# A two-block transformer stack on one core: queries and keys of the second block transposed together, doubled on the way out of PSUM

## The chip, the core and the metric

The kernel runs on one core of a Trainium2 chip. The time is the device time of one execution in microseconds (us), from three executions. The engines are TensorE (PE, with its weight loads PEld), VectorE (DVE), ScalarE (ACT), GpSimd (POOL) and SyncE (SP), which issues the DMAs. Each works through its own instructions in order and waits on semaphores for the others.

## The reference

512 tokens of width 1024 pass through a first block (two layers of feed-forward, mixing with differential attention, feed-forward) and a second block of two hybrid layers. Only the second block is touched:

```python
def hybrid_layer(x, mem, norm_g, w_in, w_out, mem_norm_g, w_mem_kv, qk_g):
    h = rms_norm(x, norm_g)
    proj = jnp.einsum('btd,de->bte', h, w_in)
    a_q, a_k, a_v, a_g, b_q, b_k, b_v, b_g, m_q, m_g = jnp.split(proj, cuts, axis=-1)
    qa = rope(rms_norm(to_heads(a_q, N_HEADS_MOBA), qk_g[0]))
    ka = rope(rms_norm(to_heads(a_k, N_HEADS_MOBA), qk_g[1]))
    oa = from_heads(moba_attention(qa, ka, to_heads(a_v, N_HEADS_MOBA)))
    ...   # b: six dilated heads, in the same way
    mkv = jnp.einsum('bmd,de->bme', rms_norm(mem, mem_norm_g), w_mem_kv)
    m_k, m_v = jnp.split(mkv, 2, axis=-1)
    qm = rms_norm(to_heads(m_q, N_HEADS_MEM), qk_g[4])
    km = rms_norm(to_heads(m_k, N_HEADS_MEM), qk_g[5])
    om = from_heads(memory_attention(qm, km, to_heads(m_v, N_HEADS_MEM)))
    y = jnp.concatenate([oa * jax.nn.silu(a_g), ob * jax.nn.silu(b_g), om * jax.nn.silu(m_g)], axis=-1)
    return x + jnp.einsum('bte,ed->btd', y, w_out)
```

There are 6 + 6 + 4 heads of 64 columns, 512 tokens, 256 memory rows. Every query and key is normalized over its 64 columns, the first twelve heads' are rotated, and the scores need them with the 64 columns on the partitions.

## The kernel before

**Precision.** Every matmul operand is kept as a float32r value ("hi") and the remainder ("lo"). A product takes three matmuls (`mm3`: hi by hi, hi by lo, lo by hi; lines 56 to 58). ACT makes the hi by a cast (`hi`, line 62), DVE or POOL the lo by a subtraction (`lo`, line 67). Weights come in tiles `wf` by DMA; ACT and POOL split each half tile into `wh` and `wl`, up to three halves ahead of PE.

**Second block.** x stands transposed in SBUF, in eight tiles of 128 channels by 512 tokens. A layer (`hyb`) is a list of steps, `HYB` (line 547): `u0` to `u5` are the rope units, each the queries and keys of two heads; `u6` the queries of the four memory heads; `v` a group of four heads' values, `g` a pair's gates, `m` the memory's keys and values, `A` to `C` a quarter of the output projection. The part ahead of the first bar runs alone; each later part is blended (`blend`) with the attention of one pair of heads, in the order of `PAIRS`: after every piece of attention a few pieces of steps follow. A unit step has four pieces, a gate step two.

**A unit** (`token_major`, then `put_unit`). 96 matmuls of 256 columns give, in two PSUM accumulators (tag `acc`, three buffers) of 512 columns, for four groups of 128 tokens the 256 columns q, k, q, k of two heads. `put_unit` then has, traced with priority: ACT copies both accumulators to SBUF (`u`, line 715). `heads` squares them on ACT (623), sums the squares per head on DVE (624), takes the power -1/2 on POOL (`qc`, 630), and for each half multiplies `u` by a table of cosines on DVE (`m`, 636) and by one of sines on POOL (`n`, 637), and adds the two on POOL (639). For each group of 128 tokens DVE multiplies by `qc` and writes each head's 64 columns twice side by side (`m2`, 648), PE transposes the four blocks of 128 columns (653) into a PSUM tile `pt` (tag `tp`, two buffers, shared with attention), and `unit_dest` takes it out: one cast by ACT for all four, one subtraction on DVE for the keys' lo (`kl`), one for the lower half of the queries. So a query stands as hi over lo on 128 partitions and a key as hi over hi, and two matmuls make a score.

The memory queries take the same way without the rotation (the gain is multiplied in on POOL, 642), the memory keys too, with 256 rows.

**What sets the order.** The program is traced through a framework that orders each engine's instructions by trace order, by priority and by its own estimate of times; buffers from a pool are handed out as they come free. Scratch tiles of 128x512 (tag `t`) have six buffers.

Of the kernel before, what the change touches and what calls it, by code (L numbers as in the profile page):

```python
# [11 lines left out]
F = _mybir.dt.float32  # L12
# [33 lines left out]
class Kernel:  # L46
# [500 lines left out]
    HYB = 'u0 v0 g0|u1 g1|m u6|g6 g7 u2|v1 g2 A|u3 g3|u4 v2|u5 g4 g5|B C'.split('|')  # L547
# [31 lines left out]
    def hyb(self, l, hp, stats, after, late):  # L579
# [36 lines left out]
        def heads(us, nt, zz, kind, gain, dest):  # L616


            nb = nt // 2
# [11 lines left out]
            for b, u in enumerate(us):  # L631
                if kind is not None:
                    co, si = (t[:, 2 * b:2 * b + 2].unsqueeze(2).to_broadcast([P, 2, 2, 128]) for t in tabs[kind])
                    u4 = u.rearrange("p (a b c) -> p a b c", a=2, b=2)
                    m, n = scratch("m"), scratch("n")
                    nc.vector.tensor_tensor(m.rearrange("p (a b c) -> p a b c", a=2, b=2), u4, co, op=ALU.mult)
                    nc.gpsimd.tensor_tensor(n.rearrange("p (a b c) -> p a b c", a=2, b=2), u4, si, op=ALU.mult)
                    m3, n3 = (x.rearrange("p (a s c) -> p a s c", s=2, c=32) for x in (m, n))
                    nc.gpsimd.tensor_tensor(m3, m3, n3[:, :, ::-1], op=ALU.add)  # L639
                else:  # L640
                    m = scratch("m")
                    nc.gpsimd.tensor_tensor(m.rearrange("p (a c) -> p a c", c=64), u.rearrange("p (a c) -> p a c", c=64),
                                            gain.unsqueeze(1).to_broadcast([P, 8, 64]), op=ALU.mult)
                m8 = m.rearrange("p (a c) -> p a c", c=64)
                for i in range(2):
                    h4 = slice(8 * b + 4 * i, 8 * b + 4 * i + 4)
                    m2 = scratch("m2")
                    nc.vector.tensor_tensor(m2.rearrange("p (a d c) -> p a d c", a=4, d=2),  # L648
                                            m8[:, 4 * i:4 * i + 4].unsqueeze(2).to_broadcast([P, 4, 2, 64]),
                                            c[:, h4].unsqueeze(2).unsqueeze(3).to_broadcast([P, 4, 2, 64]), op=ALU.mult)  # L650
                    pt = self.ps.tile([P, 4, P], F, tag="tp", name="pt", bufs=2)
                    for j in range(4):
                        nc.tensor.transpose(pt[:, j], m2[:, j * P:(j + 1) * P], self.ident)
                    dest(pt, 2 * b + i)

        def unit_dest(qk, kl):

            def f(pt, tt):
                t = slice(tt * P, (tt + 1) * P)
                self.hi(qk[:, :, t], pt)  # L660
                self.lo(nc.vector, kl[:, :, t], pt[:, 1::2], qk[:, 1::2, t])
                self.lo(nc.vector, qk[64:P, 0::2, t], pt[64:P, 0::2], qk[64:P, 0::2, t])
            return f

        def q_dest(qk):
            def f(pt, tt):
                t = slice(tt * P, (tt + 1) * P)
                self.hi(qk[:, :, t], pt)
                self.lo(nc.vector, qk[64:P, :, t], pt[64:P], qk[64:P, :, t])
            return f  # L670

        def k_dest(kh, kl):
# [4 lines left out]
            return f  # L677

# [31 lines left out]
        def put_unit(p):  # L710
            def f(pv):
                us = []
                for b in range(2):
                    u = scratch("u")
                    nc.scalar.copy(u, flat(pv[b]))  # L715
                    us.append(u)
                qk = hp.tile([P, 4, T], R, tag="qk", name="qk", bufs=2)
                if p < 6:
# [437 lines left out]
```

## Time and profile before

| | us |
|---|---|
| median of 3 executions | 2536.55 |
| lowest, highest | 2532.47, 2537.79 |
| the profiled execution | 2537.32 |
| its span | 2535.5 |
| PE busy in the span | 2443.4 (96%) |
| POOL, ACT, DVE busy | 1531.0, 1058.1, 932.3 |
| second block within the span | from about 1885 to 2535 |

The span is the time from the first to the last instruction. Busy time is the union of an engine's instructions. A row of waits says which engine's instruction stood idle and what ended that; a row of the timeline gives start, duration, engine, line, tile written and read, and in brackets the idle time ahead of it. PEclk is the clock that TensorE was granted, as a share of 2.4 GHz; 0.50 is its other level, 1.2 GHz.

### The profile page before, as it was taken

The page shows a single profiled execution, that of the slowest core. Times are in us where ns is not written, and L with a number is a line of the kernel's source. Part 1 is how long each engine was busy: PE and PEld are TensorE (multiplying, and loading weights), DVE is VectorE, ACT ScalarE, POOL GpSimd, SP SyncE. Part 2 cuts the span into 40 slices and gives each one's busy share as a digit, 9 for nine tenths or more (in the row PEclk, how much of TensorE's full clock was granted, in tenths as well). Part 3 has the DMA queues.
Part 4 walks back from the last instruction along what each step waited for, and adds up shares of the span by engine and source line. Part 5 has one row for each costly group of instructions (what it writes and reads, how often), then busy time and mean ns, then how long its engine had stood idle before and what let it go on. Part 6 is the DMA issues. An engine that isn't in the chain of part 4 may idle for free.

```text
span 2535.5 us, 32847 instructions
## 1 busy us (share of the span) xinstructions
PE 2443.4 (96%) x12390; PEld 2065.3 (81%) x12390; DVE 932.3 (37%) x1607; ACT 1058.1 (42%) x2009; POOL 1531.0 (60%) x1184
## 2 busy tenths in 40 slices
PE   8999999999999999999999999999997999889988
PEld 6888888887888888888888888888886888778886
DVE  3111114772111111111127841111165766765777
ACT  4333335643333333333336543333445554555553
POOL 7777555547666557666546377766655535555543
PEclk9999999999999999999999999999998999989999
DMA  3323332223333332333332223333332212122211
GB/s 127 100 92 100 92 110 92 81 73 94 98 100 96 93 100 93 100 95 94 97 109 80 81 83 100 93 98 94 98 100 78 69 51 67 53 65 84 67 59 67
DMA packets 66975, 223.37 MB, mean 88 GB/s; under 512 B 7680, under 2 KB 10880, under 8 KB 66816
## 3 DMA queue, kind: packets, MB, share of 16 engines
q1 hardware_dynamic: 66816, 221.27, 28.0%
q8 instruction: 98, 1.61, 0.3%
q14 instruction: 61, 0.50, 0.1%
HBM read 219.14 MB, written 2.10 MB: 87 GB/s over the span
## 4 chain that ended last, share of the span: by engine, by line
PE 80%; DVE 9%; POOL 5%; issue 3%; ACT 2%; DMA 1%; SPq 0%; POOLq 0%; ACTq 0%; DVEq 0%
PE acc L56 18%; PE acc L57 18%; PE acc L58 18%; PE up L56 6%; PE up L58 6%; PE up L57 6%; DVE m L648 2%; POOL wl L67 1%; POOL ss L126 1%; POOL qc L630 1%; POOL m L639 1%; PE o L824 1%; DVE AL L67 1%; PE pt L875 1%; PE sc L814 1%
## 5 line engine op out<-in xcount | busy, mean ns | idle before, releaser
L67 POOL TENSOR_TENSOR wl<-wf,wh 128x512 fp32r<-128x512 f32 (+1 forms) x814 | 1055.0, 1298 | 889.3 <-ACT wh L62 878.1
L62 ACT CAST wh<-wf 128x512 fp32r<-128x512 f32 (+1 forms) x814 | 497.3, 611 | 1113.0 <-PE acc L57 691.2
L56 PE MATMUL acc<-xh,wh 128*128 128x512 f32 x992 | 388.7, 392 | 6.7 <-ACT wh L62 5.7
L57 PE MATMUL acc<-xl,wh 128*128 128x512 f32 x992 | 390.5, 394 | 4.6 <-DVE xl L114 4.3
L58 PE MATMUL acc<-xh,wl 128*128 128x512 f32 x992 | 388.4, 392 | 0.1
L57 PE MATMUL up<-xl,wh 128*128 128x512 f32 x704 | 274.2, 390 | 0.0
L56 PE MATMUL up<-xh,wh 128*128 128x512 f32 x704 | 274.2, 390 | 0.0
L58 PE MATMUL up<-xh,wl 128*128 128x512 f32 x704 | 274.0, 389 | 0.0
L57 PE MATMUL acc<-hl,wh 128*128 128x512 f32 x704 | 274.0, 389 | 0.0
L56 PE MATMUL acc<-hh,wh 128*128 128x512 f32 x704 | 274.0, 389 | 0.0
L58 PE MATMUL acc<-hh,wl 128*128 128x512 f32 x704 | 274.0, 389 | 0.0
L57 PE MATMUL acc<-wl,xh 128*128 128x256 f32 (+1 forms) x752 | 221.6, 296 | 4.8 <-POOL wl L67 4.8
L57 PEld LDWEIGHTS acc<-xl,wh 128*128 128x128 f32 x992 | 186.9, 188 | 47.1 <-DVE xl L114 10.3
L56 PEld LDWEIGHTS acc<-xh,wh 128*128 128x128 f32 x992 | 187.1, 189 | 46.3 <-ACT wh L62 5.7
L58 PE MATMUL acc<-wh,xl 128*128 128x256 f32 (+1 forms) x752 | 218.9, 293 | 0.0
L58 PEld LDWEIGHTS acc<-xh,wl 128*128 128x128 f32 x992 | 186.9, 188 | 38.1 <-POOL wl L67 0.9
L56 PE MATMUL acc<-wh,xh 128*128 128x256 f32 (+1 forms) x752 | 213.9, 294 | 3.1 <-ACT u L715 2.6
L211 DVE TENSOR_TENSOR u<-up,R 128x512 f32<-128x512 f32 x88 | 60.8, 691 | 387.3 <-PE up L58 387.3
L209 DVE TENSOR_TENSOR g<-acc,R 128x512 f32<-128x512 f32 x88 | 60.9, 692 | 381.5 <-PE acc L58 381.4
L222 DVE SCALAR_TENSOR_TENSOR x<-acc,x 128x512 f32<-128x512 f32 x32 | 22.1, 691 | 400.5 <-PE acc L58 400.5
L58 PEld LDWEIGHTS up<-xh,wl 128*128 128x128 f32 x704 | 132.3, 188 | 27.5
L57 PEld LDWEIGHTS acc<-hl,wh 128*128 128x128 f32 x704 | 132.2, 188 | 27.5
(229 smaller groups left out, 4263.1 us busy)
## 6 DMA issues: line engine op xcount, KB each, us to landing
wf<-wgu SPq DMA_DIRECT2D x175, 512.0 KB, 3.5
wf<-wdn SPq DMA_DIRECT2D x64, 512.0 KB, 3.5
wf<-w2u SPq DMA_DIRECT2D x28, 512.0 KB, 3.5
wf<-wdn SPq DMA_DIRECT2D x32, 384.0 KB, 3.0
wf<-wmi SPq DMA_DIRECT2D x20, 512.0 KB, 3.5
wf<-wmo SPq DMA_DIRECT2D x16, 512.0 KB, 3.5
wf<-w2g SPq DMA_DIRECT2D x16, 512.0 KB, 3.5
wf<-w2o SPq DMA_DIRECT2D x16, 512.0 KB, 3.5
```

What stands on the lines that cost most here:

```text
L56: mm(out, sh, mh, start=start, stop=False, **kw)
L57: mm(out, sh, ml, start=False, stop=False, **kw)
L58: mm(out, sl, mh, start=False, stop=stop, **kw)
L62: self.nc.scalar.copy(out, src)
L67: eng.tensor_tensor(out, src, hi.bitcast(F), op=ALU.subtract)
L126: eng.tensor_tensor(self.ss[:, :n], self.ss[:, :n], sq[:, :n], op=ALU.add)
L209: nc.vector.tensor_tensor(g, pg, Rb, op=ALU.mult)
L211: nc.vector.tensor_tensor(u, pu, Rb, op=ALU.mult)
L630: nc.gpsimd.tensor_tensor(c[:, :4 * nt], flat(w)[:, :4 * nt], self.mhalf[:, :4 * nt], op=ALU.pow)
L639: nc.gpsimd.tensor_tensor(m3, m3, n3[:, :, ::-1], op=ALU.add)
L648: nc.vector.tensor_tensor(m2.rearrange("p (a d c) -> p a d c", a=4, d=2), m8[:, 4 * i:4 * i + 4].unsqueeze(2).to_broadcast([P, 4, 2, 64]), ...
L814: nc.tensor.matmul(sc, q[:, t], kh[:, :n], start=first, stop=False, skip_group_check=True)
```

## The change

The queries and keys of a unit are transposed together, in half as many transposes. `heads` is split in three. `normed` squares straight from the accumulators, copies them to SBUF only for POOL's product with the sines, and reads PSUM for the product with the cosines (memory queries: for the product with the gain, now on DVE). `scaled` multiplies the 128x512 `m` by `qc` in place, without doubling. `turned` transposes four blocks of 128 columns for each 256 tokens: a block holds q and k of one head, so q comes out on partitions 0 to 63 and k on 64 to 127. The doubling is done by ACT and DVE, on 64 partitions at a time: for each half, three casts (k down, q up, k up) and three subtractions in place of one cast and two subtractions for each 128 tokens. `normed` and `scaled` are traced with priority as before; `turned` is put on a list, `later`, and traced without priority after two more pieces of steps, or at the end of the part. The memory keys keep the old form. In `HYB`, `g6 g7 u2` becomes `g6 u2 g7`.

```diff
-    HYB = 'u0 v0 g0|u1 g1|m u6|g6 g7 u2|v1 g2 A|u3 g3|u4 v2|u5 g4 g5|B C'.split('|')
+    HYB = 'u0 v0 g0|u1 g1|m u6|g6 u2 g7|v1 g2 A|u3 g3|u4 v2|u5 g4 g5|B C'.split('|')
...
-        def heads(us, nt, zz, kind, gain, dest):
+        def normed(pv, nt, zz, kind, gain):
...
-            for b, u in enumerate(us):
+            for b, src in enumerate(pv):
                 sq = scratch("sq")
-                nc.scalar.activation(sq, u, AF.Square)
+                nc.scalar.activation(sq, src, AF.Square)
...
+                m = scratch("m")
+                m8 = m.rearrange("p (a c) -> p a c", c=64)
                 if kind is not None:
+                    u, n = scratch("u"), scratch("n")
+                    nc.scalar.copy(u, src)
...
+                    nc.vector.tensor_tensor(by4(m), by4(src), co, op=ALU.mult)
+                    nc.gpsimd.tensor_tensor(by4(n), by4(u), si, op=ALU.mult)
...
-                    nc.gpsimd.tensor_tensor(m.rearrange("p (a c) -> p a c", c=64), u.rearrange("p (a c) -> p a c", c=64),
+                    nc.vector.tensor_tensor(m8, src.rearrange("p (a c) -> p a c", c=64),
                                             gain.unsqueeze(1).to_broadcast([P, 8, 64]), op=ALU.mult)
...
+        def scaled(ms):
+            for m, m8, c in ms:
+                nc.vector.tensor_tensor(m8, m8, c.unsqueeze(2).to_broadcast([P, 8, 64]), op=ALU.mult)
...
+        def turned(ms, dest):
+            for b, (m, _, _) in enumerate(ms):
+                pt = self.ps.tile([P, 2, 256], F, tag="tp", name="pt", bufs=2)
+                for h in range(2):
+                    for i in range(2):
+                        j = 2 * i + h
+                        nc.tensor.transpose(pt[:, h, i * P:(i + 1) * P], m[:, j * P:(j + 1) * P], self.ident)
+                dest(pt, slice(256 * b, 256 * b + 256))
...
-            def f(pt, tt):
-                t = slice(tt * P, (tt + 1) * P)
-                self.hi(qk[:, :, t], pt)
-                self.lo(nc.vector, kl[:, :, t], pt[:, 1::2], qk[:, 1::2, t])
-                self.lo(nc.vector, qk[64:P, 0::2, t], pt[64:P, 0::2], qk[64:P, 0::2, t])
+            def f(pt, t):
+                q, k = qk[:, 0::2, t], qk[:, 1::2, t]
+                self.hi(k[down], pt[down])
+                self.hi(q[up], pt[up])
+                self.hi(k[up], pt[down])
+                self.lo(nc.vector, kl[down, :, t], pt[down], k[down])
+                self.lo(nc.vector, q[down], pt[up], q[up])
+                self.lo(nc.vector, kl[up, :, t], pt[down], k[down])
...
+                later.append([2, lambda: turned(ms, dest)])
...
+        def due(n):
+            for e in later[:]:
+                e[0] -= n
+                if e[0] <= 0:
+                    later.remove(e)
+                    e[1]()
...
+                for _ in gen:
+                    yield
+                    due(1)
+            due(9)
```

Three places show how the order on the engines moves, all at unit 1 of the first layer (`u1`).

On ACT, before, around the copies of the unit's accumulators (`u<-acc`; `os` and `AH` are attention's, `p` its exponentials):

```order
L62 CAST AH<-pt 128x384
L62 CAST wh<-wf 128x512
L802 ACTIVATE p,l_15053<-p,m 128x512
L62 COPY os<-o 64x512
L715 COPY u<-acc 128x512 x2
L62 CAST AH<-pt 128x3x128
L623 ACTIVATE sq<-u 128x512 x2
```

and of the changed kernel:

```order
L826 ACTIVATE p,l_15037<-p,m 128x384
L62 COPY os<-o 64x512
L621 ACTIVATE sq<-acc 128x512
L62 CAST wh<-wf 128x512
L621 ACTIVATE sq<-acc 128x512
L635 COPY u<-acc 128x512
L62 CAST AH<-pt 128x3x128
L826 ACTIVATE p,l_15037<-p,m 128x512
L635 COPY u<-acc 128x512
```

The squares now come first and read the accumulators, and the second copy follows the exponential that stood ahead of both.

On POOL, before, the same unit's n, power and add (`m<-m,n`) among the weights' remainders (`wl`):

```order
L637 TENSOR_TENSOR n<-u,ts 128x512
L67 TENSOR_TENSOR wl<-wf,wh 128x512
L630 TENSOR_TENSOR qc<-qw,mhalf 128x16
L639 TENSOR_TENSOR m<-m,n 128x512
L67 TENSOR_TENSOR wl<-wf,wh 128x512
L637 TENSOR_TENSOR n<-u,ts 128x512
L639 TENSOR_TENSOR m<-m,n 128x512
```

and of the changed kernel:

```order
L639 TENSOR_TENSOR n<-u,ts 128x512
L641 TENSOR_TENSOR m<-m,n 128x512
L628 TENSOR_TENSOR qc<-qw,mhalf 128x16
L639 TENSOR_TENSOR n<-u,ts 128x512
L67 TENSOR_TENSOR wl<-wf,wh 128x512 x2
L641 TENSOR_TENSOR m<-m,n 128x512
```

The first half's add stands ahead of the power, and two weight remainders that stood between now follow the second n.

On PE, before, from the last weighted sums of pair 0 (`o`) to the memory's first matmuls (`acc<-wh,mm`); `sc` are pair 1's scores:

```order
L822 MATMUL o<-AH,v 128x128
L824 MATMUL o<-AL,v 64x128
L653 MATMUL pt<-ident,m_15298 128x128 x4
L653 MATMUL pt<-ident,m_15308 128x128 x4
L814 MATMUL sc<-qk 128x128
L815 MATMUL sc<-kl,qk 128x128
L814 MATMUL sc<-qk 128x256
L815 MATMUL sc<-kl,qk 128x256
L653 MATMUL pt<-ident,m_15323 128x128 x4
L653 MATMUL pt<-ident,m_15333 128x128 x4
```

and of the changed kernel:

```order
L848 MATMUL o<-AL,v 64x256
L662 MATMUL pt<-ident,m 128x128 x4
L56 MATMUL acc<-wh,mm 128x512
L57 MATMUL acc<-wl,mm 128x512
L56 MATMUL acc<-wh,mm 128x512
L57 MATMUL acc<-wl,mm 128x512
L838 MATMUL sc<-qk 128x128
L839 MATMUL sc<-kl,qk 128x128
L838 MATMUL sc<-qk 128x256
L839 MATMUL sc<-kl,qk 128x256
```

Four transposes take the place of eight, the memory's matmuls stand between them and the scores, and the second four follow six more of those matmuls. The weighted sums of pair 0 that stood behind the unit's end now stand ahead of it in part.

## Rows read from the trace of the kernel before

**Rows 1.** Windows: us, busy of PE, PEld, DVE, ACT, POOL, PEclk, DMA, GB/s

```profile
1500.00:1900.00 400.00, 396.93 (x1918) 334.82 (x1918) 78.43 (x126) 148.32 (x254) 268.40 (x212) 1.00 0.31 97
...
1885.00:2536.00 651.00, 581.81 (x3781) 517.77 (x3780) 445.62 (x813) 333.90 (x744) 334.40 (x236) 0.96 0.21 66
```

**Rows 2.** Waits of PE, 1885 to 2536: total us, times, longest us

```profile
PE pt L653 <- DVE m L648: 25.1, 15, 7.3
PE pt L875 <- DVE qk L67: 5.0, 5, 1.6
PE sc L814 <- DVE qk L67: 4.4, 8, 0.8
...
PE acc L56 <- ACT u L715: 3.1, 3, 1.3
```

**Rows 3.** Timeline at unit 1, layer one: start us, us, what, idle time before

```profile
1903.63 1.08 ACT L715 COPY u<-acc 128x512 f32<-128x512 f32 x2
...
1904.18 0.39 PE L58 MATMUL acc<-xh,wl 128*128 128x512 f32 x1
...
1904.41 0.39 PE L56 MATMUL acc<-xh,wh 128*128 128x512 f32 x1
...
1914.87 1.97 PE L653 MATMUL pt<-ident,m 128*128 128x128 f32 x8 [6.55 <-DVE m L648]
```

**Rows 4.** Timeline at unit 4, layer one

```profile
2092.36 1.07 ACT L715 COPY u<-acc 128x512 f32<-128x512 f32 x2
...
2093.00 0.39 PE L56 MATMUL acc<-wh,xh 128*128 128x256 f32 x1 [1.28 <-ACT u L715]
...
2102.20 0.81 PE L653 MATMUL pt<-ident,m 128*128 128x128 f32 x4 [3.88 <-DVE m L648]
```

**Rows 5.** Windows behind idle stretches, columns as in rows 1

```profile
1915.00:1925.00 10.00, 7.85 (x31) 6.58 (x32) 8.93 (x23) 6.00 (x15) 3.12 (x3) 0.50 0.15 45
...
2262.00:2273.00 11.00, 8.84 (x33) 7.27 (x33) 9.93 (x25) 6.56 (x16) 3.60 (x3) 0.50 0.17 49
2102.00:2106.00 4.00, 3.80 (x19) 3.80 (x20) 3.99 (x5) 0.59 (x1) 4.00 (x3) 0.57 0.37 134
```

**Rows 6.** Chain that ended last, one piece: start us, us, what

```profile
2367.84 0.87 PE pt L653 x8
```

**Rows 7.** Groups of PE, 1885 to 2536: count, busy us, mean ns, idle before

```profile
L653 PE MATMUL pt<-ident,m 128*128 128x128 f32 x232 | 37.9, 297 | 26.7 <-DVE m L648 25.1 <-DVE qk L67 1.5
```

**Rows 8.** Groups of DVE, 1885 to 2536

```profile
L648 DVE TENSOR_TENSOR m<-m,qc 128x512 f32<-128x512 f32 x58 | 68.5, 1219 | 31.2 <-POOL m L639 30.3 <-POOL qc L630 0.7
...
L636 DVE TENSOR_TENSOR m<-u,tc 128x512 f32<-128x512 f32 x22 | 23.8, 1080 | 2.5 <-ACT u L715 2.5
...
L67 DVE TENSOR_TENSOR qk<-pt,qk 64x256 fp32r<-64x256 f32 x46 | 19.7, 428 | 0.6
...
L786 DVE TENSOR_TENSOR gate<-acc,R 128x512 f32<-128x512 f32 x16 | 11.0, 685 | 4.1 <-PE acc L58 3.9
...
L67 DVE TENSOR_TENSOR qk<-pt,qk 64x512 fp32r<-64x512 f32 x8 | 5.4, 692 | 1.6 <-ACT qk L62 1.5
```

**Rows 9.** Groups of ACT, 1885 to 2536

```profile
L62 ACT CAST qk<-pt 128x512 fp32r<-128x512 f32 x54 | 30.9, 581 | 47.4 <-PE pt L653 47.3
...
L623 ACT ACTIVATE sq<-u 128x512 f32<-128x512 f32 x28 | 16.5, 639 | 0.2
...
L715 ACT COPY u<-acc 128x512 f32<-128x512 f32 x26 | 14.3, 589 | 4.2 <-PE acc L58 3.9
```

**Rows 10.** Groups of POOL, 1885 to 2536

```profile
L67 POOL TENSOR_TENSOR wl<-wf,wh 128x512 fp32r<-128x512 f32 x148 | 203.6, 1381 | 223.7 <-ACT wh L62 215.8 <-PE acc L58 6.9 <-POOL wl L67 0.4
L630 POOL TENSOR_TENSOR qc<-qw,mhalf 128x16 f32<-128x16 f32 x13 | 38.7, 2979 | 0.4
L637 POOL TENSOR_TENSOR n<-u,ts 128x512 f32<-128x512 f32 x22 | 33.2, 1508 | 62.7 <-DVE qs L624 41.5 <-PE acc L58 17.0 <-DVE m L648 4.2
L639 POOL TENSOR_TENSOR m<-m,n 128x512 f32<-128x512 f32 x22 | 28.7, 1304 | 0.5
```

More of the change, by code (lines that the diff above doesn't have):

```diff
@@ L656, in unit_dest @@
[L656 to L662 removed]
+                ms.append((m, m8, c[:, 8 * b:8 * b + 8]))
+            return ms
+        def scaled(ms):
+            for m, m8, c in ms:
+                nc.vector.tensor_tensor(m8, m8, c.unsqueeze(2).to_broadcast([P, 8, 64]), op=ALU.mult)
@@ new lines, in hyb @@
+        up, down = slice(0, 64), slice(64, P)
+        def turned(ms, dest):
[6 more added lines that the diff above has]
+                dest(pt, slice(256 * b, 256 * b + 256))
+        def unit_dest(qk, kl):
+            def f(pt, t):
[6 more added lines that the diff above has]
+                self.lo(nc.vector, kl[up, :, t], pt[down], k[down])
@@ L663, in unit_dest, with f @@
             return f
         def q_dest(qk):
[L666 to L669, printed above, removed]
+            def f(pt, t):
+                for j, own in enumerate((up, down)):
+                    q = qk[:, j::2, t]
+                    self.hi(q[up], pt[own])
+                    self.lo(nc.vector, q[down], pt[own], q[up])
             return f
@@ L677, in k_dest @@
             return f
+        later = []
         ops = [None] * KT
@@ L711, in f @@
             def f(pv):
[L712 to L716, printed above, removed]
                 qk = hp.tile([P, 4, T], R, tag="qk", name="qk", bufs=2)
+                ms = normed([flat(x) for x in pv], 4, zt, p // 3 if p < 6 else None, gm[:, 0])
+                scaled(ms)
                 if p < 6:
@@ L771, in mem_kv @@
                 self.mem_ops = [hp.tile([P, 4, NMEM], R, tag="kl", name=n, bufs=3) for n in ("khm", "klm")]
-                heads([u], 2, zmt, None, gm[:, 1], k_dest(*self.mem_ops))
+                (_, m8, c), = normed([u], 2, zmt, None, gm[:, 1])
+                for i in range(2):
+                    m2 = scratch("m2")
+                    nc.vector.tensor_tensor(m2.rearrange("p (a d c) -> p a d c", a=4, d=2),
+                                            m8[:, 4 * i:4 * i + 4].unsqueeze(2).to_broadcast([P, 4, 2, 64]),
+                                            c[:, 4 * i:4 * i + 4].unsqueeze(2).unsqueeze(3).to_broadcast([P, 4, 2, 64]),
+                                            op=ALU.mult)
+                    pt = self.ps.tile([P, 4, P], F, tag="tp", name="pt", bufs=2)
+                    for j in range(4):
+                        nc.tensor.transpose(pt[:, j], m2[:, j * P:(j + 1) * P], self.ident)
+                    k_dest(*self.mem_ops)(pt, i)
             yield
@@ L908, in steps @@
                 if step in "ABC":
-                    yield from self.out_part(yh, yl, "ABC".index(step), every=2)
+                    gen = self.out_part(yh, yl, "ABC".index(step), every=2)
                 else:
-                    yield from {"u": lambda: token_major(put_unit(n)), "v": lambda: token_major(put_values(n)),
-                                "g": lambda: gate(n), "m": mem_kv}[step]()
+                    gen = {"u": lambda: token_major(put_unit(n)), "v": lambda: token_major(put_values(n)),
+                           "g": lambda: gate(n), "m": mem_kv}[step]()
+                for _ in gen:
+                    yield
+                    due(1)
+            due(9)
         for _ in steps(self.HYB[0]):
```

25 lines of the change are left out of this document (5 added, 20 removed).

## The prediction

> **What bounds the kernel now.** The change touches only the second block, so I first compared stretches [rows 1]. From 1500 to 1900 us TensorE (PE) is busy 396.93 of 400 us: nothing but fewer matmuls helps there, and the diff leaves that part alone. From 1885 to 2536 it is busy 581.81 of 651 us. The other 69 us are what this change can reach, together with any PE work it removes.
>
> Second, who PE waits for there [rows 2]. The longest wait is that of the transposes (L653) for the product on VectorE (DVE) that scales a head's rows (L648): 25.1 us in 15 waits. Three more belong to the same chain: softmax transposes that wait for a PSUM buffer which the split of queries and keys still reads (5.0), scores that wait for that split (4.4), projections that wait for an accumulator until ScalarE (ACT) has copied it out (3.1). Together 37.6 us; the rest of the idle time is short waits inside attention.
>
> Third, why L648 is late [rows 3]. In the first layer's second unit (unit 1, the first being 0) ACT copies the accumulator at 1903.63, behind other work in its queue; the transposes start at 1914.87, and PE has idled 6.55 us for them. The chain from the copy to the transposes is 11.2 us, and GpSimd (POOL) holds most of it: n, a weight remainder, the power qc, the add, all in one queue. In unit 4 of that layer it is 9.8 us (2092.36 to 2102.20) [rows 4], and PE idles 1.28 and 3.88.
>
> Fourth, the clock [rows 5]. Behind the two longest idle stretches (layer one and its twin in layer two) PE runs at 0.50 of its clock, the 1.2 GHz level, for 10 and 11 us, busy 7.85 and 8.84 us of them. At 2.4 GHz that work takes half: 8.3 us are lost.
>
> **The change part by part.**
>
> Transposes. Fourteen units (six rope units and the memory queries, in two layers) go from 16 transposes to 8; the memory keys keep their 8. So 240 become 128: 112 fewer. Eight back to back take 0.87 us, 0.109 each [rows 6]; the busy time per recorded one is 37.9/232 = 0.163 [rows 7]. That is 12.2 to 18.3 us. I take 12.2, since the second figure holds the slow clock and waits for neighbours. [...]
>
> The work around them. Per rope unit DVE loses four products of 1.219 and eight splits of some 0.43, and gains two products of 1.219 and six half-height splits, priced at the 0.692 of the 64x512 form [rows 8]. Its product with the cosines now reads PSUM and not a copy: I price it like the gate product from an accumulator (0.685) instead of 1.080. With two cosine products each that is 10.5 us before, 8.0 after. [...] ACT goes from 4.8 to 5.9 us a unit (two copies, two squares, four casts out of PSUM; then six casts) [rows 9]. POOL loses the products of the memory heads with their gain, which go to DVE, and nothing else [rows 10]. DVE is busy 445.6 and ACT 333.9 of 651 us [rows 1], so all this is taken at nothing; what hides it is PE's own 582 us. If an engine's queue were the cover that fails, it would show in the next term.
>
> The waits. "Two steps later" moves only where the transposes are traced; what counts is the chain's length against the PE work that now stands ahead of them. The new chain [rows 8 to 10]: square, square, copy (0.64+0.64+0.59), n 1.51, add 1.30, qc 2.98, scale 1.22: 8.9 us at the least, and up to 11.7 where the other half's n and add stand ahead of qc on POOL. It is no shorter than the 9.8 to 11.2 seen. Its start moves: in unit 1 the attention matmuls that ACT's earlier copy needs now come before the unit's end. I count the PE work from the start of the chain to the first transposes out of the new order, with 0.23 for a 512-wide matmul [rows 3], half of it for a 256-wide one, 0.109 for a transpose.
> Unit 1, layer one: 24 gate matmuls 5.4, eleven transposes 1.2, ten weighted sums 1.15, two scores 0.46: 8.2 us of cover. Chain with one weight cast on ACT (0.59, like the copy): 9.5. Wait 1.3; the second half's add stands behind an n and two weight remainders (1.51+2x1.38), with 3.1 of cover from the first transposes on, which costs some 2.4 more. 3.7 against 6.55 before and its followers. Layer two: the attention copy first (0.58), and an n and a weight remainder ahead of qc, 12.4 against 9.7 of cover, then 1 more: 3.6.
> Unit 0: five POOL operations in a bunch; chain 2.5 on ACT, two n and two adds 5.6, qc 2.98, scale 1.22: 12.3 against 9.3 of cover; in layer two a weight remainder more, 13.7 against 12.0. Wait 3.0 and 1.7.
> Unit 4: ACT is still held by the attention copy; from there 0.58, then the shortest chain with one n more, 11.0, against 6.4 of cover. Wait 4.6 in each layer, the accumulator's part in it; 5.2 before in layer one, but less in layer two.
> Units 2, 3 and 5 have 10.9 to 12.2 of cover against 10.0 to 12.4: 0.6 in all. The memory queries have no POOL add any more and 10.5 of cover: none.
> Sum: 3.7+3.6+4.7+9.2+0.6 = 21.8 us in place of 37.6: 15.8 saved. Bounds: all 37.6 saved if the chains end in time; none saved, and even more waiting, if POOL's bunches run late everywhere (below).
>
> The clock. With waits of 1 to 3 us at unit 1 the two long slow stretches should go (8.3 back). Unit 4's wait of 4.6 us is like the one of 3.88 at 2102, behind which the clock was 0.57 for 4 us [rows 5]; a second such stretch in layer two costs some 2 us. I take 6.
>
> The reordered step (g6 u2 g7) lets a gate stand between unit 2 and the next values, so that the accumulator is free in time; part of the 3.1 us, already counted.
>
> **Sum.** The profiled execution took 2537.3 us, 0.8 above the median of 2536.55. 2537.3 - 12.2 - 15.8 - 6 = 2503.3; against the median, 2502.5.
>
> **The rivals.**
> (a) The waits vanish: all 37.6, the whole 8.3 and the 12.2: 2479. For it: DVE's and POOL's queues are lighter, and no unit's transposes are traced with priority any more. Against: POOL still does qc in 2.98 us and four products a unit.
> (b) The chain takes over: waits add up to what they were, only the transposes go: 2525. For it: the chain is no shorter.
> (c) Slower. POOL's operations of a unit now stand in one bunch, up to 8.6 us in which no weight remainder is made, and the accumulators are held by a square, a copy and a DVE product instead of one copy. If each of the twelve rope units then waits as unit 4 does, that is 4.6x12 = 55 us; break-even is 37.6+12.2 = 49.8, 4.2 a unit. At 5.4 a unit, 65 us with 8 us of slow clock kept: about 2552. Against: six of the twelve have cover as long as the chain.
> [...]
>
> **How the numbers follow.** The forecast 0.55 (2490 to 2518), (a) 0.14, (b) 0.14, (c) 0.09, (d) 0.08. The measurement can tell about 0.2%, 5 us. Faster: the forecast, (a), (b): 0.83; same 0.08; slower 0.09. The range drops (c), half of (d) and the lower part of (a): 2482 to 2532.
>
> **What would show it.** In the new trace: 128 transposes from m; PE's waits for the scaling product near 20 us and not 25.1 plus its followers; no idle stretch over 5 us and none of the 10 us at 0.50 behind unit 1; DVE busy some 30 us less in the second block. Wrong would be a wait for POOL's weight remainders in place of the transposes', more than 4 us a unit, or PE's busy time down by much less than 12 us.

## The result, and the profile after

The changed kernel takes 2490.73 us (median of 4 executions, 2488.77 to 2491.87) against 2536.15 for the kernel before (4 executions, 2532.47 to 2537.79): ratio 0.9822, 95% interval 0.9805 to 0.9839. That is 45 us less; the forecast was 34 us less, and the time lies inside the range. The profiled execution took 2488.77 us, its span is 2487.0, 48.5 us under the span before.

TensorE's waits in the second block come first, as in [rows 2], here from 1848 us on, where unit 0 of the first layer begins; the second block thus starts earlier than the 1885 from which the rows of before were read (total us, times, longest us). Before, the longest from 1848 on:

```profile
PE pt L653 <- DVE m L648: 26.4, 16, 7.3
```

And in the changed kernel:

```profile
PE pt L662 <- DVE m L650: 9.7, 6, 2.7
PE acc L56 <- ACT mm L759: 4.2, 2, 2.3
PE o L846 <- DVE os L912: 4.0, 4, 1.4
PE acc L56 <- DVE m L638: 3.8, 1, 3.8
PE o L846 <- ACT AH L62: 3.8, 5, 1.1
PE pt L877 <- DVE AL L67: 2.9, 2, 1.5
```

L662 are the new transposes, L650 the scaling in place. The wait between them is 9.7 us where 26.4 stood (25.1 from 1885 on). The waits of softmax transposes and of scores for the split of queries and keys (5.0 and 4.4 before) are gone but for 0.3. Three rows are new: the memory's matmuls wait for their operand `mm` (4.2), some of the softmax transposes (L877) for a PSUM buffer that the split of the softmax weights (`AL`) still reads (2.9), and the projections behind unit 0 of layer one (the first values) wait once, 3.8 us, for an accumulator that VectorE's cosine product (L638) still reads.

The second block's windows, before and after (us, busy of PE, PEld, DVE, ACT, POOL, PEclk, DMA, GB/s):

```profile
1848.00:2535.00 687.00, 616.63 (x4046) 550.73 (x4045) 473.82 (x854) 347.82 (x769) 362.81 (x255) 0.97 0.22 69
```
```profile
1848.00:2487.00 639.00, 592.62 (x3936) 534.23 (x3935) 449.42 (x808) 360.01 (x790) 350.24 (x249) 0.97 0.23 74
```

The block is 48 us shorter. I divide its length in three: TensorE's idle time (length less busy time); what the slow clock takes (over all windows of 1 us, the busy time times one less PEclk, which takes work at 0.50 as twice as long); and the rest, the work at full clock. Two is a little much: in the changed kernel 256-column matmuls of unit 0 start 0.21 us apart at PEclk 0.50 (1873.88 to 1876.22) and 0.12 at 1.00 (1876.61 to 1877.80), and 512-column ones of unit 1's stretch 0.43 (1918.28 to 1919.56) and 0.23 (1921.19 to 1921.88). That is 1.8 to 1.9 times as long, by which, an estimate, the column is some 6 to 13% too high. The two levels named above as 1.2 and 2.4 GHz show here as 1.2 columns a ns at 0.50, and 2.1 to 2.2 at 1.00. All kernels of this study follow in the same table, each from its profiled execution; "median" is the time over all executions. The ratios further down are each against the kernel before on the same chip, whose medians there were 2534.07 to 2536.56.

| kernel | median us | block | idle | slow clock | work |
|---|---|---|---|---|---|
| before | 2536.15 | 687 | 70.3 | 18.5 | 598.2 |
| hyb_only | 2536.04 | 688 | 70.5 | 17.5 | 600.0 |
| normed_only | 2528.38 | 677 | 60.8 | 25.7 | 590.5 |
| together_only | 2510.70 | 659 | 56.4 | 25.6 | 577.1 |
| together_now | 2510.02 | 661 | 57.3 | 21.9 | 581.8 |
| old_hyb | 2504.33 | 654 | 54.5 | 20.2 | 579.3 |
| changed | 2490.73 | 639 | 46.4 | 14.7 | 577.9 |
| transposes_twice | 2490.68 | 647 | 41.7 | 11.3 | 594.0 |
| late_old_form | 2515.35 | 664 | 53.0 | 19.3 | 591.7 |
| delay_only | 2531.27 | 684 | 69.9 | 17.0 | 597.1 |
| add_on_dve | 2478.77 | 628 | 36.5 | 11.3 | 580.1 |
| add_dve_transposes_twice | 2484.84 | 637 | 37.0 | 4.9 | 595.1 |
| add_dve_at_once | 2488.49 | 635 | 44.4 | 21.7 | 568.9 |
| no_copy | 2478.76 | 630 | 39.7 | 7.1 | 583.2 |

From before to changed: idle 23.9 less, slow clock 3.8 less, work 20.3 less. The split between the last two columns is not good to better than some 10 us, since the ends of matmuls are modelled: normed_only has 7.7 us less work than the kernel before, and add_dve_at_once 11.2 less than add_on_dve, with the same matmuls in the program; both have as much more slow clock (7.2 and 10.4).

The places of [rows 3] and [rows 4] in the changed kernel. Unit 1, layer one, timeline (start us, us, what, idle time before):

```profile
1902.90 0.60 ACT L621 ACTIVATE sq<-acc 128x512 f32<-128x512 f32 x1 [0.61 <-PE acc L58]
...
1908.24 2.91 POOL L628 TENSOR_TENSOR qc<-qw,mhalf 128x16 f32<-128x16 f32 x1
...
1912.40 1.79 DVE L650 TENSOR_TENSOR m<-m,qc 128x512 f32<-128x512 f32 x1
...
1914.33 1.09 PE L662 MATMUL pt<-ident,m 128*128 128x128 f32 x4 [0.77 <-DVE m L650]
...
1915.46 1.76 ACT L62 CAST qk<-pt 64x512 fp32r<-64x512 f32 x3 [1.28 <-PE pt L662]
...
1917.12 0.51 ACT L759 ACTIVATE mm<-mf,gc 128x256 fp32r<-128x256 f32 x1
...
1917.68 0.80 PE L56 MATMUL acc<-wh,mm 128*128 128x512 f32 x1 [2.26 <-ACT mm L759]
```

From the first square to the transposes are 11.4 us; the chain is no shorter than the 11.2 before. But TensorE has 9.61 us of work in that stretch and waits 0.77 for the transposes, where it waited 6.55 (another 1.06 are attention's waits for `AH` and `AL`). The power ends at 1911.15 and the scaling starts at 1912.40: for that 1.25 us the chain stands in VectorE's queue, behind work of a gate and of attention. Behind them ScalarE's three casts of `qk` (1.76 us) stand ahead of the memory's operand, and TensorE waits 2.26 for that: the first new wait.

Unit 4, layer one:

```profile
2076.64 1.09 ACT L621 ACTIVATE sq<-acc 128x512 f32<-128x512 f32 x2
...
2078.28 1.27 POOL L639 TENSOR_TENSOR n<-u,ts 128x512 f32<-128x512 f32 x1 [10.73 <-ACT u L635]
...
2079.63 1.30 POOL L641 TENSOR_TENSOR m<-m,n 128x512 f32<-128x512 f32 x1
...
2080.89 1.30 POOL L639 TENSOR_TENSOR n<-u,ts 128x512 f32<-128x512 f32 x1
...
2082.14 3.10 POOL L628 TENSOR_TENSOR qc<-qw,mhalf 128x16 f32<-128x16 f32 x1
...
2085.27 1.75 DVE L650 TENSOR_TENSOR m<-m,qc 128x512 f32<-128x512 f32 x1 [0.27 <-POOL qc L628]
...
2087.16 0.63 PE L662 MATMUL pt<-ident,m 128*128 128x128 f32 x4 [2.18 <-DVE m L650]
...
2088.19 1.75 DVE L650 TENSOR_TENSOR m<-m,qc 128x512 f32<-128x512 f32 x1 [1.17 <-POOL m L641]
```

GpSimd works without a gap from 2078.28 to 2085.2, and the power is its last piece ahead of the first half's scaling (the second half's add comes behind it). The transposes wait 2.18 us, where 1.28 for the accumulator and 3.88 for the scaling stood.

The clock of the changed kernel behind the waits of unit 1, and then at unit 0 of the first layer before and after (columns as above):

```profile
1913.00:1917.00 4.00, 1.65 (x9) 1.02 (x8) 3.93 (x4) 2.10 (x4) 3.99 (x3) 0.64 0.56 170
1917.00:1921.00 4.00, 3.32 (x10) 2.67 (x11) 3.89 (x7) 1.85 (x5) 0.00 (x0) 0.51 0.31 92
```
```profile
1864.00:1885.00 21.00, 18.82 (x133) 17.04 (x131) 17.70 (x23) 6.59 (x13) 17.79 (x12) 1.00 0.18 59
```
```profile
1864.00:1885.00 21.00, 17.18 (x112) 16.34 (x111) 15.83 (x21) 7.81 (x15) 14.88 (x10) 0.84 0.20 68
```

Read in windows of 1 us, the level of 0.50 shows at unit 1 from 1914 to 1921 and again from 1927 to 1932, behind the second wait for `mm`; before, it showed from 1911 to 1926, of which [rows 5] has the last ten. At unit 0 of the first layer the changed kernel lost: PEclk was 1.00 there before, and is 0.84 behind the wait of 3.8 us for the accumulator.

### The profile page after: what moved, and what is told of

Read it like the earlier page. It is cut to its first block, busy times and chain, and to the rows that moved or that the text cites. A ratio compares the mean times of both kernels' runs of the same rounds, so it can differ in the third digit from the quotient of the medians.

```text
span 2487.0 us, 32615 instructions
## 1 busy us (share of the span) xinstructions
PE 2417.5 (97%) x12278; PEld 2047.1 (82%) x12278; DVE 908.2 (37%) x1561; ACT 1070.3 (43%) x2029; POOL 1518.0 (61%) x1178
## 4 chain that ended last, share of the span: by engine, by line
PE 87%; DVE 6%; POOL 2%; ACT 2%; issue 2%; DMA 0%; SPq 0%; POOLq 0%; ACTq 0%; DVEq 0%
PE acc L56 20%; PE acc L58 20%; PE acc L57 20%; PE up L56 6%; PE up L58 6%; PE up L57 6%; POOL ss L126 1%; PE sc L838 1%; PE sc L839 1%; DVE m L650 1%; PE o L846 1%; PE o L848 1%; PE pt L899 1%; DVE kl L463 1%; PE pt L877 1%
## 5 line engine op out<-in xcount | busy, mean ns | idle before, releaser
L57 PEld LDWEIGHTS acc<-xl,wh 128*128 128x128 f32 x992 | 186.7, 188 | 48.0 <-DVE xl L114 11.1
L211 DVE TENSOR_TENSOR u<-up,R 128x512 f32<-128x512 f32 x88 | 60.8, 691 | 387.3 <-PE up L58 387.3
L56 PEld LDWEIGHTS up<-xh,wh 128*128 128x128 f32 x704 | 132.6, 188 | 27.5
```

Of the source, the lines that this page charges most:

```text
L56: mm(out, sh, mh, start=start, stop=False, **kw)
L57: mm(out, sh, ml, start=False, stop=False, **kw)
L211: nc.vector.tensor_tensor(u, pu, Rb, op=ALU.mult)
```

## The experiments

Two theories stood against each other. Mine: the chain from the accumulator to the scaled rows is as long as before, and what pays is the place of the transposes, with the transposes' own time beside it. The rival: the lighter work pays, wherever it stands.

**together_now: the changed kernel without the delay.**

```
-                later.append([2, lambda: turned(ms, dest)])
+                turned(ms, dest)
```

> The changed kernel with the transposes and the copies out of PSUM traced at once behind the scaling, inside the stretch with priority, as the kernel before had them; everything else as changed. In the changed kernel's trace TensorE's waits on the units' chain fell from 37.6 to 10.0 us, its other busy time by 16 us and the slow clock's share by 6. My theory: the later place brought the fall of the waits, the half number of transposes only the 16 us. Then the waits come back in large part (20 to 30 us), and the time is 2505 to 2520. Rival: the lighter chain (squares and cosine product straight from PSUM, fewer products on VectorE) brought it; then 2490 to 2497.

Measured: 2510.02 us (ratio to before 0.9897, 0.9884 to 0.9911). The delay is worth 19.3 us in the changed kernel, but 25 us of the 45 come without it. Not by the route that I expected:

```profile
PE pt L662 <- DVE m L650: 11.0, 11, 2.7
PE acc L56 <- ACT mm L759: 8.3, 3, 5.5
PE o L846 <- DVE os L912: 7.2, 7, 1.5
```

The wait for the scaling is hardly longer (11.0 against 9.7). TensorE's idle time rises by 10.9 us in the table, and not by 20 to 30. What comes back stands elsewhere: the memory's operand 8.3 (4.2), attention's sums `os` 7.2 (4.0), and 7 us more of slow clock. I read this as work that, traced at once and with priority, stands on ScalarE and VectorE ahead of what other steps need; no run parts the delay from the loss of the priority.

**delay_only: the kernel before with the delay.** The doubled products stay early, in the buffers of `u` and `n`:

```
-                    m2 = scratch("m2")
+                    m2 = (u, n)[i] if kind is not None else scratch("m2")
...
+            if nt == 4:
+                later.append([2, turned])
```

> The kernel before with its old form (copies first, doubled products, sixteen transposes a unit), but transposes and copies out of PSUM traced two pieces later and without priority. The doubled products stay early, in the buffers of u and n, so four scratch buffers of a unit are held longer than before. My theory (place): the waits fall as in the changed kernel and only the transposes' 16 us are missing: 2503 to 2512. Rival (the work): little changes, 2525 to 2537. A third: held scratch buffers keep the other steps waiting, above 2540.

Measured: 2531.27 us (0.9982, 0.9972 to 0.9992). That is the rival's range, and mine is missed by 19 us. The waits show why it still does not decide between the two:

```profile
PE pr L904 <- DVE rx L901: 19.2, 2, 10.6
PE acc L57 <- POOL wl L67: 8.2, 9, 1.3
PE pt L656 <- DVE qk L67: 6.7, 6, 1.5
...
PE pt L656 <- DVE u L648: 4.0, 3, 2.5
```

The wait for the scaled rows did fall, to 5.1 us (4.0 for `u`, 1.1 for `n`), but `rx`, another user of the six scratch buffers, now keeps TensorE waiting twice, 19.2 us together, at unit 1 of each layer. VectorE makes `rx` behind the unit's last scaled product, at 1924.55 in layer one, as it did in the kernel before (1919.74); with the transposes moved behind it, the wait for the chain shows there. In the changed kernel `rx` comes at 1908.32, ahead of the scaling. The form that scales in place holds two buffers instead of four, which I take to be what lets `rx` go ahead; no run parts that from the order on VectorE.

**late_old_form: the old form, all of it delayed.** It keeps the changed kernel's first part, order and list, and puts the doubled products, sixteen transposes and the old split into `turned`:

```
-            for b, (m, _, _) in enumerate(ms):
-                pt = self.ps.tile([P, 2, 256], F, tag="tp", name="pt", bufs=2)
...
+            for b, (m, m8, c) in enumerate(ms):
+                for i in range(2):
+                    m2 = scratch("m2")
...
```

> The changed kernel (normed, new order, list of two pieces) with the old way of getting queries and keys: four doubled products, sixteen transposes and the old split for a unit, all of it two pieces later and without priority, so that no scratch buffer is held longer than in the changed kernel. By my sum the 112 transposes cost 12.2: 2503, and 2503 to 2508 with the two more products a unit ahead of each transpose. By the run with each transpose issued twice (2490.7 at the median) they lie in waits that are there anyway: 2490 to 2496. Rival: four products of 1.2 us now stand straight ahead of the transposes on VectorE and TensorE waits for them: over 2510.

Measured: 2515.35 us (0.9917, 0.9904 to 0.9930), 24.6 above the changed kernel and beyond what the transposes alone explain. By the table 13.8 of it is TensorE's work, 6.6 idle time, 4.6 slow clock. The rival's number came (over 2510), but its wait for the scaled products is only 2.6 us longer than in the changed kernel (12.3 against 9.7); two rows of waits for the split of queries and keys, 9.5 us, are back too:

```profile
PE pt L666 <- DVE m L660: 12.3, 11, 2.7
...
PE pt L666 <- DVE qk L67: 4.9, 3, 2.1
PE sc L837 <- DVE qk L67: 4.6, 6, 1.5
```

So here the work of the old form, its transposes included, does cost time.

**transposes_twice: the price of 112 transposes.**

```
-                        nc.tensor.transpose(pt[:, h, i * P:(i + 1) * P], m[:, j * P:(j + 1) * P], self.ident)
+                        for _ in range(2):
+                            nc.tensor.transpose(pt[:, h, i * P:(i + 1) * P], m[:, j * P:(j + 1) * P], self.ident)
```

> The changed kernel with each of the 112 transposes of units and memory queries issued twice, the second writing the same values again: the price of 112 transposes in place, with no other engine touched. At 0.109 us each: plus 12.2, 2503. At 0.143, which is what the fall of TensorE's busy time outside the slow clock gives for each of the 112 removed: plus 16, 2507. [...] Under 2500 if transposes lie in time in which TensorE would wait anyway.

Measured: 2490.68 us, 2489.22 to 2497.59, the median of the changed kernel to 0.1 us. The groups of TensorE (count, busy us, mean ns, idle before), changed kernel and this one:

```profile
L662 PE MATMUL pt<-ident,m 128*128 128x128 f32 x112 | 17.8, 284 | 9.8 <-DVE m L650 9.7
```
```profile
L663 PE MATMUL pt<-ident,m 128*128 128x128 f32 x224 | 29.6, 277 | 11.5 <-DVE m L650 11.4
```

The transposes are there and cost 11.8 us of busy time, 0.105 each. But the run does not give their price alone, for two reasons. Of the changed kernel's two waits for `mm` (4.2 us) 0.2 is left, because the order on ScalarE moved with the transposes: at unit 1 the operand now stands ahead of the casts of `qk`, and not behind them.

```profile
1919.11 0.51 ACT L760 ACTIVATE mm<-mf,gc 128x256 fp32r<-128x256 f32 x1 [0.34 <-DMA mf<-memT]
...
1920.94 1.76 ACT L62 CAST qk<-pt 64x512 fp32r<-64x512 f32 x3
```

And the clock differs between the executions. The profiled one has a mean granted clock of 0.992 over its span, as every execution of the changed kernel has, and takes 2497.59 us; one with 0.994 takes 2493.54, and the three with 0.996 to 0.997 take 2489.22 to 2490.68. So at the same clock the doubling cost some 7 us (2497.59 against 2490.73), with 4.0 us of waits taken away beside it; at the median the higher clock gave this back.

**old_hyb: the order of steps undone.**

```
-    HYB = 'u0 v0 g0|u1 g1|m u6|g6 u2 g7|v1 g2 A|u3 g3|u4 v2|u5 g4 g5|B C'.split('|')
+    HYB = 'u0 v0 g0|u1 g1|m u6|g6 g7 u2|v1 g2 A|u3 g3|u4 v2|u5 g4 g5|B C'.split('|')
```

> The changed kernel with the old order of steps, g6 g7 u2 in place of g6 u2 g7. My prediction put it inside 3.1 us of waits for an accumulator: 2490 to 2494 here. Rival: with the later transposes the gate between unit 2 and the next values is the cover that the last transposes of that part need, then unit 2's chain shows at TensorE in both layers as unit 4's does: 2.5 to 4.5 us each, 2496 to 2500.

Measured: 2504.33 us (0.9872, 0.9859 to 0.9886), 13.6 above the changed kernel. The prediction had this inside 3.1 us, and the rival's range is passed as well. Unit 2's transposes in the first layer:

```profile
2005.15 0.63 PE L662 MATMUL pt<-ident,m 128*128 128x128 f32 x4 [0.69 <-DVE m L650]
2007.96 0.66 PE L662 MATMUL pt<-ident,m 128*128 128x128 f32 x4 [2.18 <-DVE m L650]
```

They wait 2.87 us, in the changed kernel 0.35 (in layer two 2.87 and 1.56). At the end of a part the list is emptied, so a unit that is last in its part has no delay. The memory queries (`u6`) are last in theirs in both orders; in the changed kernel their transposes, at 1971.90 and 1972.57 in layer one, do not wait. The table gives 8.1 us more idle time and 5.5 more slow clock.

**hyb_only and together_only: is that the order's own worth?** The same line of `HYB` alone in the kernel before; and the changed kernel without delay and with the old order.

> The kernel before with the new order of steps alone (g6 u2 g7). Undoing the order in the changed kernel cost 13.6 us (2504.3 against 2490.7). My theory now: that is worth only with the later transposes, because with u2 last in its part the list is emptied right behind it and unit 2 has no delay at all; in the kernel before, where transposes stand at once, the order is worth 0 to 4 us: 2531 to 2536. Rival: the order itself frees an accumulator, whatever the transposes do: 2519 to 2526.

> The changed kernel without delay and with the old order of steps: only the transposes together, with the squares and cosine product from PSUM. With the new order and without delay it was 2510.0. If the order is worth something only with the delay: 2509 to 2514. If the order has its own worth: 2519 to 2526.

Measured: hyb_only 2536.04 us (0.9999, 0.9990 to 1.0007), nothing; together_only 2510.70 (0.9901, 0.9887 to 0.9915), as without the delay but with the new order (2510.02). So the order is worth 0 to 1 us without the delay and 13.6 with it, and the delay 6.4 us with the old order and 19.3 with the new one. They are one change in two lines.

**normed_only: the first part of the change alone.** Squares and cosine product from PSUM, with the old order, old form, no delay:

```
-                nc.scalar.activation(sq, u, AF.Square)
+                nc.scalar.activation(sq, src, AF.Square)
...
-                    nc.vector.tensor_tensor(m.rearrange("p (a b c) -> p a b c", a=2, b=2), u4, co, op=ALU.mult)
+                    nc.vector.tensor_tensor(by4(m), by4(src), co, op=ALU.mult)
```

> The kernel before (old order of steps, no delay, four doubled products, sixteen transposes, old split) with the first part of the change alone: squares and the cosine product straight from PSUM, the copy behind the squares, the memory queries' gain product on VectorE. All of the change but delay and order gave 2510.7 against 2535.4. My theory: the joint transposes give most of that (16 us less of TensorE's time and half as much to be taken out of PSUM before attention can go on), this part little: 2526 to 2536. Rival: the earlier and lighter start of the chain gives most of it: 2512 to 2522.

Measured: 2528.38 us (0.9968, 0.9956 to 0.9979), 8 us of the 25; the joint transposes with their new way out of PSUM are worth the other 17.7. The wait for the scaled rows is 20.1 us here, against 25.1 before [rows 2] and 11.6 in together_only.

**add_on_dve: is GpSimd's queue the chain?**

```
-                    nc.gpsimd.tensor_tensor(m3, m3, n3[:, :, ::-1], op=ALU.add)
+                    nc.vector.tensor_tensor(m3, m3, n3[:, :, ::-1], op=ALU.add)
```

> The changed kernel with the add of the two rotary products on VectorE in place of GpSimd: two operations of 1.3 to 1.4 us a unit leave GpSimd's bunch. My theory: GpSimd's queue sets the chain's end, so the 9.7 us of waits for the scaling product fall to 2 to 5 us, and the time to 2481 to 2488. Rival: VectorE, busy 424 of 602 us there, has its own queue and the chain only changes its engine: 2490 to 2500.

Measured: 2478.77 us (0.9777, 0.9763 to 0.9791), 12 us below the changed kernel and 2 below the range that I expected. The wait for the scaling over the block, and unit 4 again:

```profile
PE pt L662 <- DVE m L650: 4.0, 7, 1.2
```

```profile
2072.50 1.08 ACT L621 ACTIVATE sq<-acc 128x512 f32<-128x512 f32 x2
...
2076.07 1.32 DVE L641 TENSOR_TENSOR m<-m,n 128x512 f32<-128x512 f32 x1
2076.80 3.35 POOL L628 TENSOR_TENSOR qc<-qw,mhalf 128x16 f32<-128x16 f32 x1
...
2080.18 3.46 DVE L650 TENSOR_TENSOR m<-m,qc 128x512 f32<-128x512 f32 x2 [1.26 <-POOL qc L628]
```

The power starts 4.30 us behind the first square (5.50 in the changed kernel) and both halves are scaled 11.1 us behind it (13.3). The wait for the scaling falls from 9.7 to 4.0 us, which is 5.7 of the 9.9 us of idle time that go; the wait for `mm` falls too, from 4.2 to 1.3. So GpSimd's queue did hold the chain, and VectorE had room.

**add_dve_at_once: the delay with the shorter chain.**

> The kernel with the add on VectorE (2478.8), with the transposes traced at once behind the scaling as in the first experiment: new order of steps, no delay. In the changed kernel that cost 19.3 us (2510.0 against 2490.7). My theory: the later place is cover for the chain, so with a chain shorter by two operations on GpSimd a part of that cover is not needed: the loss is 5 to 14 us, 2484 to 2493. Rival: the later place is worth its 19 us however long the chain is, because what it takes away is other steps' waiting behind the copies out of PSUM with priority on ScalarE and VectorE: 2495 to 2500.

Measured: 2488.49 us (0.9815, 0.9802 to 0.9829). The delay is worth 9.7 us here, half of the 19.3, as my theory has it. Its reason is not borne out by the waits:

```profile
PE pt L662 <- DVE m L650: 9.0, 7, 3.2
PE o L846 <- DVE os L912: 5.6, 4, 1.4
PE acc L56 <- ACT mm L759: 5.2, 1, 5.2
```

From 1885 on, the delay takes 5.5 us off the wait for the scaling with the short chain (9.0 to 3.5), and only 1.3 with the long one (11.0 to 9.7). Of the waits for `mm` it takes 3.9 and 4.1. So the shorter chain does not need less cover in this sense, and why the delay is worth half as much stays open.

**add_dve_transposes_twice: the price again, with fewer waits to hide in.**

> The kernel with the add on VectorE (2478.8), and each of the 112 transposes issued twice. In the changed kernel the same doubling left the median where it was (2490.7), although TensorE's busy time outside the slow clock rose by 16 us: idle time and slow clock fell in its place. My theory: that needs waits to fill, and here the waits are shorter (33 us of idle time against 43, 10 us of slow clock against 12), so a part shows: 2485 to 2495. If transposes are still free: 2477 to 2483.

Measured: 2484.84 us (0.9797, 0.9784 to 0.9810): 6.1 us for 112 transposes. The work is up by 15.0 us, idle time is the same, the slow clock 6.4 us less. Less than half of the 15.0 us is seen even here, and what disappears is put down to the clock: the mean granted clock is 0.995 to 0.997 in the four executions, and 0.993 to 0.995 in those of add_on_dve. Here too ScalarE's order moved: at unit 1 `mm` now stands between the casts of the two halves, and not behind all six.

**no_copy: only the power left on GpSimd.** On top of add_on_dve, the product with the sines on VectorE, from PSUM, and no copy on ScalarE:

```
-                    u, n = scratch("u"), scratch("n")
-                    nc.scalar.copy(u, src)
+                    n = scratch("n")
...
-                    nc.gpsimd.tensor_tensor(by4(n), by4(u), si, op=ALU.mult)
+                    nc.vector.tensor_tensor(by4(n), by4(src), si, op=ALU.mult)
```

> The kernel with the add on VectorE, and the product with the sines on VectorE too, read from PSUM: no copy on ScalarE any more, and on GpSimd only the power is left of a unit. VectorE gets 44 products of 0.68 us more than in the changed kernel's copy of the work, GpSimd loses 22 of 1.3 us, ScalarE 22 of 0.6. My theory: GpSimd's queue held the chain; the power now starts at once, the chain is some 2 us shorter, the 3.5 us of waits for the scaling product go, with some of the slow clock: 2470 to 2477. Rival: VectorE, with 431 of 591 us busy, now delays softmax and splits: 2479 to 2490.

Measured: 2478.76 us (0.9773, 0.9760 to 0.9786): no gain over add_on_dve, and between the two ranges expected. The chain's wait does fall, and others take its place (from 1885 on):

```profile
PE o L847 <- DVE AL L67: 4.9, 6, 3.1
...
PE pt L876 <- DVE AL L67: 3.5, 3, 1.5
...
PE pt L661 <- DVE m L649: 1.5, 2, 0.7
```

1.5 us are left for the scaling, where add_on_dve has 3.5 in this stretch (from 1848 on 2.9 and 4.0), while the remainders of the softmax weights (`AL`, on VectorE) are late, 8.4 us in these rows. The units' chain has ceased to be what TensorE waits for most. The two fastest versions are this one and add_on_dve.

## Why the prediction was right, and where its steps were off

**What bounds the kernel.** Right: 24 us of idle time, 4 of slow clock and 20 of TensorE's work went, all in the second block. But the prediction read the block from 1885 on and took the stretch up to 1900 as untouched; unit 0 of the first layer stands there from 1848 on, and it is where the changed kernel lost.

**Transposes, 12.2 us.** The count held: 112 at L662 and 16 for the memory keys, from 240. Priced by doubling they are 11.8 us in their own group, and 15.0 to 16.1 in the table's column of work; the fall between the two traces is larger, 39.2 to 20.2 us in the groups, because transposes at the slow clock went too (eight took 1.97 us at unit 1 [rows 3], at PEclk 0.50, and 1.03 us of busy time at 2367.68, at 1.00; 0.87 of that stands in the chain [rows 6]). One transpose is 277 to 284 ns long in the groups, but each adds only 0.105 us, since the next starts before the last has ended. What the step had wrong is that TensorE's work adds to the time in full: the doubling cost some 7 us at the same clock and nothing at the median in the changed kernel, and 6.1 with the shorter chain, with ScalarE's order moved in both.

**The work around them, taken at nothing.** This is the term that was furthest off. Without the delay and the new order the lighter work gives 25.4 us (together_only), where the sum had the 12.2 of the transposes alone. 8 us come with the squares and the cosine product from PSUM (normed_only), by an earlier or by a lighter start of the chain; no run parts the two. The other 17.7 come with the joint transposes and their way out of PSUM. The single prices were near: the cosine product from PSUM takes 674 ns, priced at 685; a half-height split 694, priced at 692; the product that scales in place 1372, not 1219. VectorE is busy 24 us less, not 30. The 1080 ns of the cosine product from SBUF [rows 8] is a mean of two kinds: 0.69 us at 1904.25, with GpSimd idle, and 1.78 at 2016.10, with GpSimd at work throughout. From PSUM it took 0.68 beside GpSimd's work (1905.62). The memory keys' product from SBUF (L789), with GpSimd idle, takes 688 ns.

**The waits, 37.6 to 21.8.** They fell further. Of the chain's waits 13.8 are left: 9.7 for the scaling, 3.8 for an accumulator, 0.3 at scores; the 4.2 for `mm` come on top. Against the forecast that is 6.5 less at unit 1 and 4.8 less at unit 4, and 1.8 more at unit 0 and 1.6 more at unit 2 and at scores. By places:
- Unit 1: the chain was set at 9.5 us and took 11.4, the cover at 8.2 and was 9.61; the difference, forecast 1.3, is 1.8 (0.77 at the transposes, the rest at attention). The further 2.4 did not come at the second half's transposes but as the memory's matmuls' waits, which the prediction had not seen. In layer two no transpose waits, forecast 3.6: from the attention copy on the chain took 13.0 (forecast 12.4) and the cover was 11.4 (9.7), and the 1.65 between them stands at attention's `AH` and `AL`.
- Unit 4: chain 11.1 from the attention copy (forecast 11.0), cover 7.20 (6.4). The idle time is 3.9 us, as forecast 4.6, but only 2.18 of it is at the transposes. The rest is attention waiting for `os` and `AH`. It did so before as well, but its longest wait for `AH` there was 0.35 and is now 1.12: ScalarE's squares and first copy of the unit (2076.64 to 2078.2) stand ahead of that cast.
- Unit 0: 3.82 and 2.66 where 3.0 and 1.7 stood. In layer one it is the accumulator held by square, copy and product, the mechanism of rival (c), at one place of twelve; the transposes, for which the 3.0 was forecast, do not wait there, so that the number is near by luck. With the slow clock this made the changed kernel 1 us later than before at 1886 us.
- Unit 2: 0.35 and 1.56, where units 2, 3 and 5 had 0.6 in all.
- The 9.4 us of attention waiting for the split (softmax transposes and scores) went but for 0.3, as forecast.

**The clock, 6 us.** 3.8 over the block; 6.5 from 1885 on, less 2.7 at unit 0. At the 1.8 to 1.9 measured in place of two, the 8.3 us behind [rows 5] were 7.4 to 7.9, an estimate. The number is near, the places are not: the long stretches at the lower level behind unit 1 got shorter in both layers, but did not go.

**The order of steps, counted within 3.1 us.** This step failed: 13.6 us. I read it as room for an accumulator, and missed that the list of late transposes is emptied at the end of each part, so that without a step behind unit 2 the delay does not exist there. The diff showed it; the sum did not ask it. The sum did not suffer, since it counted unit 2's cover in the new order.

So the mechanism was right in part. The later place, with the order that it needs, is worth 20.0 us (together_only to the changed kernel), near the 21.8 that the sum had for waits and clock together, though it comes at other places than forecast. The lighter work gave twice its term, and is the larger part of the 45. Idle time fell 23.9 and not 15.8, work 20.3 and not 12.2. Of the work, 12 to 16 us are the transposes; of the last 4 to 8 no run shows the cause. normed_only has 7.7 less work with all transposes in place, but as much more slow clock, and the split between these two columns is no better than that.

## What to carry to other kernels

Work that is moved later pays only if something stands behind it: look where a queue of delayed work is emptied (a unit that is last in its part had no delay, 13.6 us), and at what the other engines' queues then hold first. Before counting an engine's saved work into a forecast in full, ask whether that engine waits near by and at which clock it runs: 112 transposes more were 15 to 16 us of work and, in time, nothing to 7 us. Do not take the work of the engines around it at nothing because they are far from busy: the lighter way gave 25.4 us where the transposes alone were put at 12.2. When a chain is the bound, shorten it on the engine that holds it longest: one add moved from GpSimd to VectorE gave 12 us.

## What the runs showed of the hardware that was not expected

With more work on TensorE its granted clock was higher in both doublings. With each transpose issued twice the slow clock took 11.3 us in place of 14.7, and 4.9 in place of 11.3 where the add is on VectorE. The mean granted clock of the executions was 0.992 to 0.997 in place of 0.992, and 0.995 to 0.997 in place of 0.993 to 0.995. Behind unit 1 of layer one, add_on_dve and then add_dve_transposes_twice (columns as above):

```profile
1917.00:1921.00 4.00, 2.53 (x7) 2.09 (x8) 3.88 (x6) 2.53 (x6) 1.28 (x1) 0.62 0.24 48
1921.00:1925.00 4.00, 4.00 (x12) 3.26 (x11) 2.61 (x10) 2.92 (x9) 1.80 (x3) 0.53 0.31 115
```
```profile
1917.00:1921.00 4.00, 2.45 (x18) 1.80 (x16) 3.89 (x7) 2.67 (x5) 0.00 (x0) 1.00 0.58 185
1921.00:1925.00 4.00, 3.28 (x15) 2.11 (x13) 3.88 (x7) 3.95 (x9) 1.52 (x2) 1.00 0.01 2
```

The second kernel has more matmuls in these windows (33 against 19) in less busy time, with PEclk at 1.00. It comes to this place 3.0 us later, so its windows begin a little earlier in the work. In windows of 1 us, TensorE idles 2.41 us from 1916 to 1919 in the first kernel, and PEclk is 0.50 from 1918 on. In the second it idles 1.56 us from 1919 to 1921. Ahead of that it is busy 1.00 in each window from 1915 to 1919, where the first has 0.76 and 0.68 in the two ahead of 1916. Which of these kept the clock up, no run tells.

From 1848 on, the same add took 1392 ns on GpSimd in the changed kernel and 1056 on VectorE in add_on_dve, while the power on GpSimd went from 2991 to 3258 ns beside it.
